# Stores of the pairs' results, the dilated attention's outputs and its statistics move from SyncE to GpSimd

## Chip, cores and metric

One core of a Trainium2 chip runs the whole program in one launch. The metric is the device time in microseconds (us), from start to end of an execution. The engines are TensorE (PE, matmuls), VectorE (DVE), ScalarE (ACT), GpSimd (POOL) and SyncE (SP). In this kernel SP starts nearly every transfer (DMA); it computes nothing.

## The reference, cut to what matters

```python
D_MODEL, SEQ, BATCH = 1024, 1024, 1
DIL_CONFIGS = ((128, 1), (512, 4), (2048, 16))   # three head groups of 4 heads, 64 channels a head
...
h = rms_norm(x, norm_w) * (1 + scale(c)) + shift(c)
proj = h @ w_in          # q,k,v,z,beta,a of mixer A; q,k,v,z of mixer B; gates g_A, g_B
...
o_a = gated_delta_rule(q_dn, k_dn, v_dn, g, beta)             # chunks of 64, 8 heads of 128
y_a = (rms_norm(o_a, dn_norm_w) * silu(za)) @ w_proj_a
...
for gi, (win, dil) in enumerate(DIL_CONFIGS):                 # mixer B: causal dilated windows
    o_g, lse_g = dilated_window_attention(qb[group], kb[group], vb[group], win, dil)
w_g = softmax(lse over the three groups)
y_b = (o_b * w_g * silu(zb)) @ w_proj_b
...
merged = sigmoid(ga) * y_a + sigmoid(gb) * y_b
x = x + gate * (merged @ w_out)
return rms_norm(x, final_norm_w)
```

All data are float32, 1024 tokens of 1024 channels.

## The kernel before

**Arithmetic.** Channels lie on the 128 partitions, tokens along the free dimension. Products of float32 matrices are split: `split` writes a rounded high part with ACT (a copy) and a low part with DVE (source minus high part), and PE makes three products (high by high, low by high, high by low).

**Buffers.** `big` holds [128, 1024] tiles, `mid` [128, 512] tiles, `wr` raw weights and `wh` split weights, all as rings of slots; `pj` and `sb` are PSUM tiles. A load that takes a slot waits until the slot's last reader is done.

**Who sets the order.** A list scheduler in Python (`Sched`) runs while the program is built. Each piece of work is a generator ("stream") with a priority. `book` keeps a modelled clock for each engine, and `run` steps the stream of the highest priority that is ready by PE's modelled clock. So the order in which instructions are written, on all engines, follows from the costs in `book`. On the chip each engine takes its instructions strictly in that order, and waits by semaphores. A changed cost in `book` can thus reorder PE, DVE, ACT and SP, though the same instructions are issued.

**The part around the change**, in the order of time:

1. Pairs (`PAIRS`, seven of them, "a" for mixer B's queries, "b" keys, "z" gates): each projects two tiles of 128 channels. `block_sink` stores each half tile [128, 512] to DRAM: `qb_d` and `kb_d` (rows `qbd`, `kbd`), `z_d` (`zd`). In the second and third head group the store also permutes tokens, in pieces of 512 x 1 x 128 or 1024 x 1 x 64.
2. Attention units (`attn_unit`, 24 of them): SP loads queries, keys and values; PE makes scores; DVE masks them and takes the row maximum; ACT takes exponentials with their sums; PE transposes; ACT copies; PE multiplies by the values; DVE copies the output; SP stores it to `og_d` (`ogd`, 128 KB). Row maxima and sums collect in `st_a` (`sta`); `attn_group` stores them after the group's last unit to `st_d` (`std`): one store for the first group, four for the second, one for the third.
3. `combine` (three): loads the statistics, forms the groups' softmax weights on DVE and ACT, transposes them and stores them to `fg_d`.
4. `yb_split` (six "slabs" of 128 channels, two per head group): loads `ogd`, `zd` and the weights (`mid<-fgd`); two half products weights x output, one whole product with z (with permuted tokens in the groups 2 and 3), then `split`. The results are the second projection's moving tiles.
5. The first projection (y_A by `w_proj_a`), eight tiles of eight steps; at each tile's end `pa_out` multiplies by a gate on DVE, `big<-big,pj`. Then the second (y_B by `w_proj_b`), eight tiles of six steps, one per slab. Weights of both are loaded and split meanwhile (`wr`, `wh`). In the last tile of the first projection the slots of its moving tiles come free step by step.

All instructions are issued through one helper, so every row of the profile has line L129; rows are told apart by engine and tile names.

Of the kernel before, what the change touches and what calls it, by code (L numbers as in the profile page):

```python
# [15 lines left out]
P = 128  # L16
# [17 lines left out]
HALVES = (slice(0, 512), slice(512, 1024))  # L34
# [13 lines left out]
def _free(ap):  # L48
    n = 1
    for s in list(ap.shape)[1:]:  # L50
        n *= s
    return n
# [83 lines left out]
class Sched:  # L136
# [19 lines left out]
    def book(self, e, op, out, a, k):  # L156
        n = _free(a[1] if op == "tensor_reduce" else out)
        done = self.cur.done
        others = max([t for q, t in done.items() if q != e], default=0.0)
        start = max(self.clk[e], self.clk["pe"], others)  # L160
        if e == "pe":
            start = self.clk["pe"]
            if op == "transpose":
                c = 109
            else:
                r = k.get("rhs", a[2] if len(a) > 2 else None)
                if r.dtype == F32R:
                    c = max(107, n / 2.4 + 2)
                elif r.shape[0] <= 64:
                    c = 30 if out.shape[0] == 32 else 60 if out.shape[0] == 64 else n / 1.1  # L170
                else:
                    c = max(214, n / 0.6) if n > 8 else 60
            end = start + c
            self.clk["pe"] = end
            hop = 190
        elif e == "dma":
            b = n * 4 * out.shape[0] * (2 if out.shape[-1] < P else 1)
            end = max(self.clk[e] + max(470, b / 360), max(self.clk["pe"], others) + 1100 + b / 360)
            self.clk[e] = end
            hop = 950  # L180
        else:
            if e == "act":
                c = n / 1.2 + (215 if "accum_out" in k else 95)
                f = TABLE.get(k.get("func", a[2] if len(a) > 2 else None))
                if f and f != self.table:
                    self.table = f
                    c += 1280
            elif e == "dve":
                c = n / 0.96 + 65
                if op == "tensor_scalar":  # L190
                    c = n / 1.92 + 130
                elif op == "scalar_tensor_tensor" and n > 8:
                    c += 60
                elif op == "reciprocal":
                    c = n * 6.2 + 70
            else:
                c = n * 2.3 + 50 if op == "tensor_tensor" else n * 1.27
                if k.get("op") == OP.pow:
                    c = n * 165 + 300
                elif n == 8 * P and k.get("op") == OP.mult:  # L200
                    c = 1900
            end = start + c
            self.clk[e] = end
            hop = 130
        done[e] = end + hop
        self.cur.last = max(self.cur.last, end + hop)
# [79 lines left out]
def hybrid_block_kernel(ctx: ExitStack, tc: tile.TileContext, x, c, norm_w, ada_w, ada_b, w_tiles, w_vb0, w_vb1,  # L286
# [3 lines left out]
    pe, act, dve, pool, sp = S.pe, S.act, S.dve, S.pool, S.sp  # L290
# [60 lines left out]
    og_d = [dp.tile([P, T], F32, name=f"ogd{i}") for i in range(6)]  # L351
# [5 lines left out]
    st_d = dp.tile([T, 3, 8], F32, name="std")  # L357
# [579 lines left out]
    def block_sink(dst, ev, func=None, scale=1.0, g=0):  # L937

        left = [2, 2]
        r_ = (1, 4, 8)[g]  # L940

        def sink(r, q, src):
            if func is not None:
                act.activation(src, src, func, scale=scale)
                yield
            if g:
                u_ = 512 // r_
                sp.dma_start(dst[r].rearrange("p (r u) -> p r u", r=r_)[:, :, q * u_:q * u_ + u_],
                             src.rearrange("p (r u) -> p r u", r=r_))
            else:  # L950
                sp.dma_start(dst[r][:, HALVES[q]], src)
            left[r] -= 1
            if not left[r]:
                S.set(ev[r])

        sink.r = r_
        return sink
# [606 lines left out]
    def attn_unit(g, i2, ti):  # L1564

        i0 = 2 * i2
        kf = max(i0 - 1, 0) if g == 0 else i0
        n_ = i0 + 2 - kf
        buf, sm2 = yield from big.many(2)
        qt, kt = buf[:, 0:256], buf[:, 256:256 + n_ * P]  # L1570
        v3 = buf[:, 640:640 + n_ * P].rearrange("p (a f) -> p a f", f=P)
        sp.dma_start(qt, qb_d[2 * g + ti][:, i0 * P:(i0 + 2) * P])
        sp.dma_start(kt, kb_d[2 * g + ti][:, kf * P:(i0 + 2) * P])
        if g == 0:
            src = vb_d[g].rearrange("(i p) f -> p i f", p=P)[:, kf:kf + n_]
        elif g == 1:
            src = vb_d[g].rearrange("(b p r) f -> r p b f", b=2, r=4)[i2]
        else:
            src = vb_d[g].rearrange("(p r) f -> p r f", r=8)[:, i0:i0 + 2]
        sp.dma_start(v3, src[:, :, ti * P:(ti + 1) * P])  # L1580
        yield
        tiles = []
        for i in (i0, i0 + 1):
            prev = (g == 0 and i > 0) or (g == 1 and i % 2 == 1)
            tiles.append((i, i % 2, (i - 1 if prev else i) - kf, 256 if prev else 128))
        sms = [sm2[:, sl] for sl in HALVES]
        pbs = yield from sb.many(2)
        for i, a, k0, nk in tiles:
            for hd in range(2):
                r = slice(64 * hd, 64 * hd + 64)  # L1590
                pe.matmul(pbs[hd][:, a * 256:a * 256 + nk], qt[r, a * P:(a + 1) * P], kt[r, k0 * P:k0 * P + nk], start=True,
                          stop=True)
        yield
        for hd in range(2):
            h4 = 2 * ti + hd
            sm = sms[hd]
            for i, a, k0, nk in tiles:
                msk = amask2 if g == 2 else amask if nk == 256 else amask[:, P:2 * P]
                dve.tensor_tensor_reduce(sm[:, a * 256:a * 256 + nk], pbs[hd][:, a * 256:a * 256 + nk], msk, -0.125, 3e38,
                                         op0=OP.add, op1=OP.min, accum_out=st_a[g][:, i, h4, 0:1])  # L1600
            sb.put()
            yield
            for i, a, k0, nk in tiles:
                s_ = sm[:, a * 256:a * 256 + nk]
                act.activation(s_, s_, AF.Exp, bias=st_a[g][:, i, h4, 0:1], scale=-1.0,
                               accum_out=st_a[g][:, i, h4, 1:2])
        yield
        pts = []
        for hd in range(2):
            pb = yield from sb.get()  # L1610
            n = 0
            for i, a, k0, nk in tiles:
                for b in range(nk // P):
                    pe.transpose(pb[:, n * P:(n + 1) * P], sms[hd][:, a * 256 + b * P:a * 256 + (b + 1) * P], ident)
                    n += 1
            yield
            pt = sms[hd]
            act.activation(pt[:, 0:n * P], pb[:, 0:n * P], AF.Copy)
            sb.put()
            pts.append(pt)  # L1620
        yield
        pb = yield from sb.get()
        n = 0
        for i, a, k0, nk in tiles:
            nb = nk // P
            for b in range(nb):
                for hd in range(2):
                    vv = v3[:, k0 + b, hd * 64:hd * 64 + 64]
                    pe.matmul(pb[64 * hd:64 * hd + 64, a * P:(a + 1) * P], vv, pts[hd][:, n * P:(n + 1) * P],
                              start=b == 0, stop=b == nb - 1)  # L1630
                n += 1
        yield
        big.put()
        dve.tensor_copy(pts[0][:, 0:2 * P], pb[:, 0:2 * P])
        sb.put()
        yield
        sp.dma_start(og_d[2 * g + ti][:, 2 * i2 * P:2 * (i2 + 1) * P], pts[0][:, 0:2 * P])
        big.put()
        pend[g] += 1
        if pend[g] == 8:  # L1640
            S.set(ev_og[g])
# [9 lines left out]
    def attn_group(g):  # L1651
        yield ev_og[g]
        sg = st_a[g]
        if g == 0:
            sp.dma_start(st_d.rearrange("(i p) g n -> p i g n", p=P)[:, :, 0], sg.rearrange("p i h s -> p i (h s)"))
        elif g == 1:
            dv = st_d.rearrange("(b p r) g n -> r p b g n", r=4, b=2)
            s4 = sg.rearrange("p (r b) h s -> p r b (h s)", b=2)
            for r in range(4):
                sp.dma_start(dv[r, :, :, 1], s4[:, r])  # L1660
        else:
            sp.dma_start(st_d.rearrange("(p i) g n -> p i g n", p=P)[:, :, 2], sg.rearrange("p i h s -> p i (h s)"))
        S.set(ev_sg[g])

    ev_sg = [Event() for _ in range(3)]
# [415 lines left out]
```

## Time and profile before

| | |
|---|---|
| time, median of 3 runs | 1279.53 us (1276.94 to 1280.24) |
| profiled execution | 1279.4 us, span 1277.7 us, granted clock 0.995 |
| PE busy | 1252.2 us (98%), 7302 matmuls |
| DVE, ACT, POOL busy | 766.9, 497.9, 173.9 us |
| stores of this change | 12 `qbd` and 12 `kbd` and 4 `zd` of 256 KB, 24 `ogd` of 128 KB, 6 `std` of 8 or 32 KB |

Busy times are shares of the span. A timeline row reads: start, duration, engine, line, operation, output <- inputs, partitions x elements, how many in a row, and in brackets the idle time of the engine before it with what ended it. PE has records with modelled ends, and a few may be missing. "SPq" is SP issuing a transfer. A row of windows gives each engine's busy time in a stretch.

### The profile page before, as it was taken

What the parts mean: (1) busy time and instruction counts of PE and PEld (TensorE: products, weight loads), DVE (VectorE), ACT (ScalarE), POOL (GpSimd) and SP (SyncE); (2) the same over time, 40 slices, a digit from 0 to 9 for tenths busy, and PEclk for the clock granted to TensorE, in tenths of its full rate; (3) what the DMA queues carried; (4) which work ended last, traced back from release to release, by engine and by line L of the source; (5) the groups of instructions that cost most, each with busy time, mean ns of one, the idle gap of its engine ahead of it and who ended that gap; (6) DMA issues with size and microseconds to landing.
All of it is one profiled execution on the core that took longest, in us unless ns stands there. A gap on an engine that the chain in (4) does not pass through costs nothing.

```text
span 1277.7 us, 19213 instructions
## 1 busy us (share of the span) xinstructions
PE 1252.2 (98%) x7302; PEld 1030.8 (81%) x7302; DVE 766.9 (60%) x1528; ACT 497.9 (39%) x1079; POOL 173.9 (14%) x128
## 2 busy tenths in 40 slices
PE   7999999999999999999999999999999999999997
PEld 3689888988888978888888888887777678878886
DVE  5845893457874367864579834555555546655533
ACT  5525622346223345233462335325555852122211
POOL 4700300033001022000320002300000000002400
PEclk9999999999999999999999999999999999999999
DMA  9534433143322262341343222645455758843422
GB/s 356 200 109 148 120 92 88 67 155 114 112 75 75 73 209 65 102 115 69 107 127 103 83 76 78 225 149 156 145 137 149 251 178 255 231 162 113 143 94 83
DMA packets 112558, 172.03 MB, mean 135 GB/s; under 512 B 41009, under 2 KB 72913, under 8 KB 112466
## 3 DMA queue, kind: packets, MB, share of 16 engines
q1 hardware_dynamic: 112322, 170.55, 42.4%
q8 instruction: 57, 0.93, 0.3%
q14 instruction: 35, 0.29, 0.1%
q10 hardware_dynamic: 144, 0.26, 0.1%
HBM read 123.40 MB, written 47.37 MB: 134 GB/s over the span
## 4 chain that ended last, share of the span: by engine, by line
PE 88%; DVE 3%; DMA 3%; ACT 2%; issue 2%; POOL 1%; SPq 0%; POOLq 0%; ACTq 0%; DVEq 0%
PE pj L129 67%; PE sb L129 22%; DVE big L129 2%; ACT big L129 1%; DMA wr<-in_w_out_dram 1%; DMA big<-kbd 1%; POOL big L129 1%; DMA big<-gd 0%; ACT wh L129 0%; DVE mid L129 0%; DVE wh L129 0%; DMA wr<-in_w_pa_dram 0%; POOL wh L129 0%; ACT L129 0%; SPq L129 0%
## 5 line engine op out<-in xcount | busy, mean ns | idle before, releaser
L129 PE MATMUL pj<-big,wh 128*128 128x512 f32 x3356 | 825.2, 398 | 0.8 <-DVE big L129 0.5
L129 PEld LDWEIGHTS pj<-big,wh 128*128 128x128 f32 x3356 | 617.2, 189 | 131.9 <-issue 9.9
L129 ACT ACTIVATE wh<-wr 128x1024 fp32r<-128x1024 f32 (+3 forms) x99 | 97.5, 985 | 239.7 <-PE pj L129 223.1
L129 DVE TENSOR_TENSOR wh<-wr,wh 128x1024 fp32r<-128x1024 f32 (+3 forms) x96 | 115.2, 1200 | 64.2 <-ACT wh L129 64.0
L129 ACT ACTIVATE big<-big 128x1024 f32<-128x1024 f32 (+2 forms) x77 | 74.1, 969 | 187.2 <-DVE big L129 133.3
L129 PE MATMUL pj<-wh,big 128*128 128x256 f32 (+2 forms) x702 | 110.6, 308 | 0.5 <-POOL wh L129 0.3
L129 PE MATMUL sb<-big,wh 128*128 128x512 f32 x368 | 105.1, 423 | 0.0
L129 PEld LDWEIGHTS pj<-wh,big 128*128 128x128 f32 x702 | 96.2, 189 | 6.2 <-POOL wh L129 0.7
L129 DVE SCALAR_TENSOR_TENSOR big<-pj,cw,big 128x1023 f32<-128x1023 f32 (+2 forms) x72 | 92.1, 1279 | 1.7
L129 PEld LDWEIGHTS sb<-big,wh 128*128 128x128 f32 x368 | 66.9, 190 | 21.1 <-issue 8.4
L129 DVE TENSOR_TENSOR big<-big,big 128x1024 f32<-128x1024 f32 (+4 forms) x44 | 57.8, 1316 | 25.9 <-ACT big L129 18.8
L129 PE MATMUL sb<-sq,big 128*128 128x128 f32 x464 | 67.9, 278 | 3.0 <-ACT sq L129 2.2
L129 PEld LDWEIGHTS sb<-sq,big 128*128 128x128 f32 x464 | 63.4, 193 | 8.8 <-ACT sq L129 3.1
L129 POOL TENSOR_TENSOR wh<-wr,wh 128x1024 fp32r<-128x1024 f32 x3 | 9.1, 3036 | 348.8 <-ACT wh L129 348.8
L129 ACT ACTIVATE big<-sb 128x512 f32<-128x512 f32 (+2 forms) x80 | 40.9, 522 | 39.6 <-PE sb L129 39.5
L129 DVE SCALAR_TENSOR_TENSOR sq<-sq,gsm,sb 128x128 f32<-128x128 f32 x48 | 16.6, 345 | 63.4 <-PE sb L129 62.2
L129 DVE CUSTOM_DVE_ANT_0 big<-sb,cst 128x128 f32<-128x128 f32 (+1 forms) x96 | 29.0, 348 | 39.7 <-PE sb L129 39.7
L129 PEld LDWEIGHTS sb<-cst,big 128*128 128x128 f32 x268 | 33.9, 145 | 22.7 <-DVE rstd L129 6.8
L129 PE MATMUL sb<-cst,big 128*128 128x128 f32 x268 | 43.5, 284 | 8.0 <-DVE rstd L129 4.9
L129 PE MATMUL pj<-big,big 128*128 128x512 f32 x210 | 49.2, 390 | 0.0
L129 ACT ACTIVATE mid<-sb 128x512 f32<-128x512 f32 (+3 forms) x48 | 24.0, 500 | 60.9 <-PE sb L129 60.5
L129 DVE TENSOR_TENSOR mid<-big 64x31 f32<-64x31 f32 (+15 forms) x124 | 41.2, 332 | 8.4 <-POOL big L129 4.9
(140 smaller groups left out, 1283.5 us busy)
## 6 DMA issues: line engine op xcount, KB each, us to landing
wr<-in_w_tiles_dram SPq DMA_DIRECT2D x64, 512.0 KB, 4.2
big<-in_ada_w_dram SPq DMA_DIRECT2D x24, 512.0 KB, 9.0
big<-in_x_dram SPq DMA_DIRECT2D x16, 512.0 KB, 5.2
gd<-big SPq DMA_DIRECT2D x16, 512.0 KB, 2.9
big<-gd SPq DMA_DIRECT2D x16, 512.0 KB, 5.2
big<-grow SPq DMA_DIRECT2D x8, 512.0 KB, 5.7
vtd<-big SPq DMA_DIRECT2D x8, 512.0 KB, 2.6
big<-vtd SPq DMA_DIRECT2D x32, 128.0 KB, 4.5
```

What stands on the lines that cost most here:

```text
L129: r = f(*a, **k)
```

## The change

58 stores are issued by POOL instead of SP: the pairs' 28, the units' 24 and the six of the statistics. `book` gets a branch for transfers on POOL: 1100 ns of the queue for an issue, landing 3000 ns and the bytes at 360 per ns after the start. Before, such a store was booked on the SP queue with that queue's cost.

```diff
@@ Sched.book
-        if e == "pe":
+        if e == "pool" and op == "dma_start":
+            self.clk[e] = start + 1100
+            end = start + 3000 + n * 4 * out.shape[0] / 360
+            hop = 950
+        elif e == "pe":
@@ block_sink
-                sp.dma_start(dst[r].rearrange("p (r u) -> p r u", r=r_)[:, :, q * u_:q * u_ + u_],
+                pool.dma_start(dst[r].rearrange("p (r u) -> p r u", r=r_)[:, :, q * u_:q * u_ + u_],
                              src.rearrange("p (r u) -> p r u", r=r_))
             else:
-                sp.dma_start(dst[r][:, HALVES[q]], src)
+                pool.dma_start(dst[r][:, HALVES[q]], src)
@@ attn_unit
-        sp.dma_start(og_d[2 * g + ti][:, 2 * i2 * P:2 * (i2 + 1) * P], pts[0][:, 0:2 * P])
+        pool.dma_start(og_d[2 * g + ti][:, 2 * i2 * P:2 * (i2 + 1) * P], pts[0][:, 0:2 * P])
@@ attn_group (three places, alike)
-            sp.dma_start(st_d..., sg...)
+            pool.dma_start(st_d..., sg...)
```

The counts of PE, DVE and ACT instructions stay. Their order changes from the third pair (about 867 us of the trace) up to the second projection's first tile (about 1124 us), and is alike before and behind.

SP's queue near the end of the attention units, before. `ogd` are output stores, `qbd`, `kbd` and `vbd` a unit's loads, `yad` loads of mixer A's output.

```order
L129 DMA ogd_190<-big_8942 128x256
L129 DMA big_9102<-qbd_179 128x256
L129 DMA big_9102<-kbd_185 128x256
L129 DMA big_9102<-vbd_119 128x2x128
L129 DMA mid_9128<-yad_126 128x512
L129 DMA mid_9129<-yad_126 128x512
L129 DMA ogd_191<-big_8978 128x256
L129 DMA big_9152<-qbd_179 128x256
L129 DMA big_9152<-kbd_185 128x256
```

Each unit's loads stand there behind an output store of an earlier unit. POOL's queue in the same part, after:

```order
L129 DMA zd_168<-mid_8651 128x512
L129 DMA zd_169<-mid_8846 128x512
L129 DMA zd_168<-mid_8799 128x512
L129 DMA ogd_189<-big_8638 128x256
L129 DMA ogd_189<-big_8686 128x256
L129 DMA ogd_190<-big_8733 128x256
L129 DMA zd_169<-mid_8719 128x512
L129 DMA std<-sta_104 128x2x8 x4
L129 DMA ogd_190<-big_8910 128x256
```

The output stores now stand among other stores only, and SP's queue holds loads there.

DVE at the last tile of the first projection, before. `pj_9742` is that tile (its row is `pa_out`), `ogd`'s slab 4 is `big_9714` with its z in `big_9715`, slab 5 `big_9769` with `big_9778`; `wh_9822` is a weight split.

```order
L129 TENSOR_TENSOR big_9714<-mid_9761,big_9714 128x512
L129 TENSOR_TENSOR big_9715<-big_9715,big_9714 128x8x128
L129 TENSOR_TENSOR big_9805<-big_9715,big_9804 128x1024
L129 SCALAR_TENSOR_TENSOR big_9740<-big_9740,pj_9742 128x1024
L129 TENSOR_TENSOR big_9769<-mid_9781,big_9769 128x512
L129 TENSOR_TENSOR wh_9822<-wr_9686,wh_9821 128x768
L129 TENSOR_TENSOR big_9769<-mid_9828,big_9769 128x512
L129 TENSOR_TENSOR big_9778<-big_9778,big_9769 128x8x128
L129 TENSOR_TENSOR big_9865<-big_9778,big_9864 128x1024
```

The same place after; slab 4 is `big_9756` with z in `big_9757`, slab 5 `big_9783` with `big_9784`, the tile `pj_9728`, the weight split `wh_9816`.

```order
L129 SCALAR_TENSOR_TENSOR big_9726<-big_9726,pj_9728 128x1024
L129 TENSOR_TENSOR wh_9816<-wr_9678,wh_9815 128x768
L129 TENSOR_TENSOR big_9783<-mid_9787,big_9783 128x512
L129 TENSOR_TENSOR big_9756<-mid_9805,big_9756 128x512
L129 TENSOR_TENSOR big_9757<-big_9757,big_9756 128x8x128
L129 TENSOR_TENSOR big_9853<-big_9757,big_9852 128x1024
L129 TENSOR_TENSOR big_9783<-mid_9843,big_9783 128x512
L129 TENSOR_TENSOR big_9784<-big_9784,big_9783 128x8x128
L129 TENSOR_TENSOR big_9865<-big_9784,big_9864 128x1024
```

Slab 4's second half product, its whole product and its split moved from ahead of the tile's gate multiply to behind it. SP's loads for these slabs, with the semaphores each waits for, before:

```order
L129 DMA big_9714<-ogd_190 128x1024 [waits DMAHW7_49]
L129 DMA big_9715<-zd_172 128x1024 [waits DMAHW0_49,DVE_49]
L129 DMA big_9769<-ogd_191 128x1024 [waits DMAHW7_49,PE_49]
L129 DMA mid_9828<-fgd_195 64x512 [waits DMAHW4_49]
L129 DMA wr_9846<-in_w_pb_dram 128x768 [waits DMAHW6_49,DVE_49]
```

and after:

```order
L129 DMA big_9756<-ogd_190 128x1024 [waits DMAHW6_49,PE_49]
L129 DMA big_9757<-zd_172 128x1024 [waits DMAHW7_49,PE_49]
L129 DMA big_9783<-ogd_191 128x1024 [waits DMAHW3_49,DMASW7_49,PE_49]
L129 DMA wr_9832<-in_w_pb_dram 128x768 [waits DMAHW2_49,DVE_49]
L129 DMA mid_9843<-fgd_195 64x512 [waits DMAHW3_49]
```

The loads of slab 4 wait for PE after the change, and the weight load stands ahead of the last load of weights `fgd` (the rows between are left out).

More of the change, by code (lines that the diff above doesn't have):

```diff
@@ L1654, in attn_group @@
         if g == 0:
-            sp.dma_start(st_d.rearrange("(i p) g n -> p i g n", p=P)[:, :, 0], sg.rearrange("p i h s -> p i (h s)"))
+            pool.dma_start(st_d.rearrange("(i p) g n -> p i g n", p=P)[:, :, 0], sg.rearrange("p i h s -> p i (h s)"))
         elif g == 1:
@@ L1659, in attn_group @@
             for r in range(4):
-                sp.dma_start(dv[r, :, :, 1], s4[:, r])
+                pool.dma_start(dv[r, :, :, 1], s4[:, r])
         else:
-            sp.dma_start(st_d.rearrange("(p i) g n -> p i g n", p=P)[:, :, 2], sg.rearrange("p i h s -> p i (h s)"))
+            pool.dma_start(st_d.rearrange("(p i) g n -> p i g n", p=P)[:, :, 2], sg.rearrange("p i h s -> p i (h s)"))
         S.set(ev_sg[g])
```

## Prediction

> **What bounds the kernel now.** I read the page's busy times, its chain and its DMA queues first.
>
> ```profile
> PE 1252.2 (98%) x7302; PEld 1030.8 (81%) x7302; DVE 766.9 (60%) x1528; ACT 497.9 (39%) x1079; POOL 173.9 (14%) x128
> ...
> q1 hardware_dynamic: 112322, 170.55, 42.4%
> ...
> PE 88%; DVE 3%; DMA 3%; ACT 2%; issue 2%; POOL 1%; SPq 0%; POOLq 0%; ACTq 0%; DVEq 0%
> ```
>
> TensorE (PE) is busy for 98% of the span and carries 88% of the chain. The change neither adds nor removes a matmul, so it can only win or lose PE's waits and what the clock does after them. SyncE's queue (SPq) has 0% of the chain: its issues as such bound nothing. So I looked next for PE's waits in the stretch that is put in another order, from the third pair (about 867 us) to the first output tile of the second projection (about 1124 us). First its list of waits for 860 to 1062 us (us in total, times, longest), then rows of PE's timeline.
>
> ```profile
> PE sb L129 <- DMA big<-kbd: 2.5, 4, 1.8
> PE sb L129 <- ACT big L129: 1.3, 2, 1.0
> ```
>
> ```profile
> 1016.17 0.71 PE L129 MATMUL sb<-cst,big 128*128 128x128 f32 x2 [1.04 <-ACT big L129]
> ...
> 1028.73 1.13 PE L129 MATMUL sb<-big 64*128 64x128 f32 x8 [1.76 <-DMA big<-kbd]
> 1029.79 4.17 PE L129 MATMUL pj<-big,wh 128*128 128x512 f32 x12
> 1033.89 0.71 PE L129 MATMUL sb<-big 64*128 64x128 f32 x8
> ...
> 1039.75 3.01 PE L129 MATMUL pj<-big,wh 128*128 128x512 f32 x12
> ...
> 1070.33 53.16 PE L129 MATMUL pj<-big,wh 128*128 128x512 f32 x232
> 1124.02 11.18 PE L129 MATMUL pj<-big,wh 128*128 128x512 f32 x48 [0.53 <-DVE big L129]
> ```
>
> Two facts carry everything below. The attention stage holds 2.5 + 1.3 = 3.8 us of PE waits, four of them for the load of an attention unit's keys. And PE waited 0.53 us at 1124.02, for the last split of an attention slab on VectorE (DVE).
>
> A wait also costs clock. After the 1.76 us, 12 matmuls took 4.17 us where 12 of the same form take 3.01, and 8 took 1.13 where 8 take 0.71: 1.16 + 0.42 = 1.6 us. The windows show it as the granted clock (behind POOL's "0.00 (x0)" stand the clock, the share of the 16 DMA engines and GB/s):
>
> ```profile
> 1024.00:1028.00 4.00, 2.71 (x18) 1.85 (x16) 1.81 (x3) 1.92 (x4) 0.00 (x0) 1.00 1.04 378
> 1028.00:1032.00 4.00, 3.27 (x13) 2.68 (x14) 2.14 (x10) 2.28 (x8) 0.00 (x0) 0.61 0.82 252
> 1032.00:1036.00 4.00, 4.00 (x25) 3.05 (x24) 1.37 (x9) 2.78 (x11) 0.00 (x0) 0.96 0.86 275
> ```
>
> The clock is 0.61 in the 4 us after that wait and 0.96 in the next. GpSimd (POOL) is at 0.00 in all three: it is free for the stores.
>
> **Part 1: 58 issues leave SP and join POOL.** What the queue held up:
>
> ```profile
> SPq L129 <- DVE big L129: 44.7, 16, 7.7
> 1021.69 0.85 SPq L129 DMA_DIRECT2D big<-kbd  x1
> 1025.00 0.32 SPq L129 DMA_DIRECT2D ogd<-big  x1
> 1048.94 0.52 SPq L129 DMA_DIRECT2D std<-sta  x1
> 1053.74 3.50 SPq L129 DMA_DIRECT2D mid<-std  x6
> 1056.94 0.85 DVE L129 TENSOR_TENSOR mid<-mid 128x32 f32<-128x32 f32 x5 [4.30 <-DMA mid<-std]
> 1080.20 1.22 DVE L129 TENSOR_TENSOR big<-big,big 128x1024 fp32r<-128x1024 f32 x1 [1.12 <-ACT big L129]
> L129 POOL TENSOR_TENSOR wh<-wr,wh 128x1024 fp32r<-128x1024 f32 x3 | 9.1, 3036 | 348.8 <-ACT wh L129 348.8
> ```
>
> An issue took SP 0.32 (an output store) to 0.52 us (a statistics store), so 58 of them free some 23 us of SP, none of it PE's. Larger is the order: between 790 and 1060 us SP stood 44.7 us waiting for DVE's `big` results with loads behind it; after the change these waits stand on POOL, with only other stores behind them. No row shows what one issue costs POOL. The nearest from below is SP's 0.32, from above POOL's longest elementwise row, 3.04 us; I take 1 us, near SP's row, since an issue passes no data through the engine. What would a late store delay? The last ones are the longest link: statistics store (1048.94), their loads (1053.74), the combination on DVE (1056.94), the first slab's split (1080.20). PE reads that slab first at the second projection's start, 32 matmuls before its wait at 1124.02, that is 1123.49 - 32 x 53.16/232 = 1116.2 us, 36 us after the split. So even 3.04 us more on the last output store, the statistics store and a landing each are hidden: 0. If a store were 10 us late or more, the chain of part 3 would start late too. For the attention units' loads the stores of their pair lie many matmuls ahead, so 0 there as well; this is the cover the third rival takes away.
>
> **Part 2: the attention stage's waits.** Loads no longer queue behind stores, so the key loads could come earlier. Against it stands the stretch where PE waited (chain; DMA in 1014 to 1032 us; the same load over the whole run):
>
> ```profile
> 1021.69 6.90 DMA big<-kbd
> ```
>
> ```profile
> q1 hardware_dynamic: 4007, 6.02, 97.0%
> big<-kbd SPq DMA_DIRECT2D x4, 128.0 KB, 4.7
> ```
>
> ```profile
> big<-kbd SPq DMA_DIRECT2D x18, 128.0 KB, 3.1
> ```
>
> The load behind the 1.76 us was issued at once, at 1021.69, 7 us ahead of its use, and took 6.90 us to land, because the transfers of that stretch fill 97% of the 16 engines; the four there took 4.7 in the median against 3.1 overall. The same bytes go through the same stretch after the change. The ends are: all 3.8 + 1.6 = 5.4 us won, or one landing of 6.90 instead of 3.1 more on the path, 3.8 us lost. I take -2.0: nearer to a gain, since SP carries loads alone, but well under half of it, since the 97% stays and PE's order puts three units' score matmuls close together.
>
> Here the Trainium skill, "DMA: Bandwidth & Descriptors", section "Issuing engines are not separate DMA queues", says that transfers issued from several engines interleave on the same 16 engines and that a second issuer saves only issue time. The trace agrees as far as it goes: 97% busy, with a wait that no issue caused. By the rule alone this part would be 0 and the sum 2.0 higher.
>
> **Part 3: the last two attention slabs.** This is the term that decides. In the new order the loads of slab 4 wait for PE, which has first to read tiles of the last tile of the first projection; before, they waited for none. So the whole of slab 4's product and split, and one more half product, now stand on DVE behind the gate multiply of that tile (`pa_out`), which waits for PE; before, slab 4 was finished ahead of it. Durations, from DVE and one ACT row before:
>
> ```profile
> 1109.56 2.17 DVE L129 TENSOR_TENSOR big<-big,big 128x1024 f32<-128x1024 f32 x1
> 1112.91 1.23 DVE L129 TENSOR_TENSOR big<-big,big 128x1024 fp32r<-128x1024 f32 x1 [1.18 <-ACT big L129]
> 1115.97 1.22 DVE L129 SCALAR_TENSOR_TENSOR big<-big,pj 128x1024 f32<-128x1024 f32 x1 [1.84 <-DMA big<-gd]
> 1117.11 0.69 DVE L129 TENSOR_TENSOR big<-mid,big 128x512 f32<-128x512 f32 x1
> 1117.71 0.95 DVE L129 TENSOR_TENSOR wh<-wr,wh 128x768 fp32r<-128x768 f32 x1
> 1118.70 0.69 DVE L129 TENSOR_TENSOR big<-mid,big 128x512 f32<-128x512 f32 x1
> 1119.43 2.18 DVE L129 TENSOR_TENSOR big<-big,big 128x1024 f32<-128x1024 f32 x1
> 1122.73 1.23 DVE L129 TENSOR_TENSOR big<-big,big 128x1024 fp32r<-128x1024 f32 x1 [1.13 <-ACT big L129]
> ```
>
> ```profile
> 1121.64 1.06 ACT L129 ACTIVATE big<-big 128x1024 fp32r<-128x1024 f32 x1 [5.27 <-DVE big L129]
> ```
>
> Before, from the gate multiply's start (1115.97) to the end of the last split (1123.96): 8.0 us. After, step by step from start to start: gate multiply 1.14, weight split 0.99, half product 0.60, half product 0.73, slab 4's product 2.21, ACT's copy 1.09, slab 4's split 1.23, half product 0.73, slab 5's product 2.21, copy 1.09, split 1.23: 13.25 us. PE already waited before, so the difference, 13.25 - 8.0 = 5.3 us, is all PE's: it would come in four pieces. Slab 4's high part is there 6.7 us after the multiply's start, and PE wants it after 24 matmuls (5.5 us): 1.2. Its low part comes 1.2 us later, when PE has done two more matmuls (0.5): 0.7. Slab 5's high part comes 4.0 after that, against four matmuls (0.9): 3.1. The last low part adds 0.8. Together 5.8 in place of 0.53. The multiply itself starts when PE ends the tile in both kernels (1116.2 by the count above, against 1115.97), so what part 2 wins moves the chain with it and doesn't shorten the wait. Ends: 3.4, if both products took the 1.23 us of a row without strides; 8.2, if one load of the chain lands 2.9 us late (a weight tile's issue, which waits for DVE's weight split, now stands ahead of the last two small loads on SP).
>
> **Part 4: clock.** The 3.1 us piece of that wait is longer than the 1.76 us that cost 1.6 us of clock: +1.6 (ends 0, since the 1.04 us wait at 1016.17 was followed by no such row, and 2).
>
> **Sum.** 0 - 2.0 + 5.3 + 1.6 = +4.9 us on the profiled execution's 1279.4 us (span 1277.7 and 1.7 around it): 1284.3 us. That execution lies 0.13 us under the median of the runs, 1279.53, so no correction. After 1124 us PE has a single wait of 0.31 us, and what follows hangs on PE's own progress: I let the delay stand to the end.
>
> **Rivals.**
> 1. The attention waits all go, and little comes in their place (no change). Part 2 is then -5.4, the sum 0 - 5.4 + 5.3 + 1.6 = +1.5, or 0 without the clock loss: 1279 to 1281 us. For it: SP waited 44.7 us ahead of loads. Against: the 97%.
> 2. Faster: the slab chain costs at most 1 us. This decides once DVE reaches slab 4's product before PE ends the last tile; then part 3 is under 1 us, part 4 is 0, and -5.4 + 1 gives 1275. For it: DVE has idle time up to the gate multiply. Against: DVE runs in order, and the product stands behind that multiply in the program.
> 3. Stores by GpSimd land late, and the loads of queries and keys that follow them too (slower by more). If POOL needs its upper 3.04 us for each, the ten stores piled up where the first split rows and the second group's statistics meet take 30 us instead of 10, and the last units' work waits for buffers that stores hold: three waits of 1.76 us are 5.3, and the sum 1289 to 1290. Against: POOL is empty there. The Trainium skill, "SBUF — State Buffer", section "SBUF: two separate sides", would push that way: it tells that DMAs of GpSimd have their descriptors written by its own cores, which VectorE's two-port operations lock out of SBUF (620 ns became 3100 ns). No run here shows a DMA of GpSimd yet.
>
> **How the numbers follow.** A measurement of this kernel tells about 0.3% (3.8 us) from no change. My forecast, slower by about 5, gets 0.45; rival 3 0.12; rival 1 0.30; rival 2 0.13. So slower 0.57, same 0.30, faster 0.13. The likeliest case alone reaches from 1282 (part 3 at 3.4) to 1287 (part 2 at 0 and the rest as taken: +6.9). The range for 8 in 10 takes rival 1 in on one side and rival 3 on the other: 1277 to 1290.
>
> **What the profile after would show.** Part 1: a GpSimd DMA queue, 58 POOL issue rows of about 1 us, and no SP row that waits for DVE with loads behind. Part 2: fewer than 3.8 us of PE waits between 860 and 1062 us, but not none, with key loads at over 4 us where the engines are full. Part 3: PE waits of 5 to 6 us in four pieces for DVE and ACT `big` in the first tile of the second projection, and two products of 2.2 us after the gate multiply. Part 4: a granted clock near 0.6 for some 4 us behind them. I am wrong if slab 4's product starts ahead of that multiply, if the attention stage loses all its waits, or if POOL's issues take 3 us.

## The result and the profile after

The changed kernel takes 1292.18 us (median of 6 runs, 1289.74 to 1295.32) against 1279.63 us before (median of 6 runs, the three of the table above among them): 12.6 us slower, ratio 1.010 with a 95% interval of 1.0083 to 1.0116. The forecast of 1284.3 us had the direction; the time lies above its range. The profiled execution took 1289.98 us, span 1287.8, granted clock 0.990.

From the page after: busy times, the two dynamic DMA queues, the chain.

```profile
PE 1257.3 (98%) x7302; PEld 1033.1 (80%) x7302; DVE 767.4 (60%) x1528; ACT 498.3 (39%) x1079; POOL 210.9 (16%) x186
...
q1 hardware_dynamic: 91426, 159.96, 38.9%
q0 software_dynamic: 3584, 10.59, 2.6%
...
PE 90%; DVE 3%; DMA 2%; ACT 2%; issue 1%; POOL 1%; SPq 0%; POOLq 0%; DVEq 0%; ACTq 0%
```

The stores moved: GpSimd has 58 instructions and 37 us more, and a queue of its own (q0). Its queue has 0% of the chain. PE has the same 7302 matmuls, but 5.1 us more busy time: the matmuls ran slower.

Where do the 10.1 us between the two profiled spans (1277.7 and 1287.8) come from? Four events stand alike in both traces and cut the span: a PE row near 451 us that waits 1.80 us for ACT `sq` (the program is the same up to 867 us), and DVE's gate multiplies of the first projection's last tile and of the second projection's first and second tile. These rows, of after first, then of before (its multiply at 1115.97 stands in the prediction):

```profile
451.81 0.49 PE L129 MATMUL sb<-sq,big 128*128 128x128 f32 x2 [1.80 <-ACT sq L129]
1118.03 1.22 DVE L129 SCALAR_TENSOR_TENSOR big<-big,pj 128x1024 f32<-128x1024 f32 x1 [2.95 <-PE pj L129]
1133.56 1.22 DVE L129 SCALAR_TENSOR_TENSOR big<-big,pj 128x1024 f32<-128x1024 f32 x1 [2.17 <-PE pj L129]
1142.83 1.22 DVE L129 SCALAR_TENSOR_TENSOR big<-big,pj 128x1024 f32<-128x1024 f32 x1 [4.43 <-PE pj L129]
```

```profile
451.39 0.49 PE L129 MATMUL sb<-sq,big 128*128 128x128 f32 x2 [1.80 <-ACT sq L129]
1125.25 1.22 DVE L129 SCALAR_TENSOR_TENSOR big<-big,pj 128x1024 f32<-128x1024 f32 x1 [1.29 <-PE pj L129]
1133.42 1.22 DVE L129 SCALAR_TENSOR_TENSOR big<-big,pj 128x1024 f32<-128x1024 f32 x1 [3.34 <-PE pj L129]
```

| stretch | before | after | difference |
|---|---|---|---|
| start to the PE row near 451 us | 451.39 | 451.81 | +0.42 |
| to the first projection's last gate multiply ("attention stretch") | 664.58 | 666.22 | +1.64 |
| to the second projection's first one ("slab stretch") | 9.28 | 15.53 | +6.25 |
| to its second one | 8.17 | 9.27 | +1.10 |
| to the end of the span | 144.3 | 145.0 | +0.7 |

So 7.35 of 10.1 us arise where the last two attention slabs meet the second projection, and 1.64 in the attention stretch.

**The attention stretch after.** PE's timeline, then PE's list of waits for 860 to 1062 us:

```profile
1016.71 1.23 PE L129 MATMUL sb<-big 64*128 64x128 f32 x8 [3.40 <-DMA big<-kbd]
...
1019.31 1.23 PE L129 MATMUL sb<-big 64*128 64x128 f32 x8 [0.33 <-DMA big<-kbd]
```

```profile
PE sb L129 <- DMA big<-kbd: 3.7, 2, 3.4
PE sb L129 <- ACT big L129: 0.5, 1, 0.5
```

The four waits for keys (2.5 us) became two (3.7 us), one of them 3.40 us long, and 8 score matmuls behind each took 1.23 us (0.71 at full clock). Why the keys were late shows in SP's queue (timeline) and in its waits between 995 and 1018 us:

```profile
1001.84 4.41 SPq L129 DMA_DIRECT2D wr<-in_w_pa_dram  x2
...
1006.78 0.42 SPq L129 DMA_DIRECT2D big<-kbd  x1
...
1010.48 0.50 SPq L129 DMA_DIRECT2D big<-kbd  x1
...
1013.31 0.80 SPq L129 DMA_DIRECT2D big<-kbd  x1
```

```profile
SPq L129 <- DVE wh L129: 11.1, 2, 7.4
```

SP no longer stands behind stores here. It stands behind two loads of weights that wait for a slot, which DVE's weight split frees (`DVE wh`, 11.1 us in two waits). Behind them came three units' loads in a bunch, while the DMA engines were full (their share was 0.95 and 1.03 in 1008 to 1016, and it stayed there; windows, the last three columns are the clock, the DMA share and GB/s):

```profile
1016.00:1020.00 4.00, 2.96 (x18) 2.40 (x20) 2.06 (x10) 2.06 (x10) 0.00 (x0) 0.53 1.08 388
1020.00:1024.00 4.00, 4.00 (x23) 2.88 (x21) 2.64 (x12) 4.00 (x16) 0.00 (x0) 0.62 1.03 389
```

**The slab stretch after.** PE's timeline, DVE's, and the windows:

```profile
1124.64 0.73 PE L129 MATMUL pj<-big,wh 128*128 128x512 f32 x2 [1.22 <-ACT big L129]
1125.90 1.20 PE L129 MATMUL pj<-big,wh 128*128 128x512 f32 x4 [0.52 <-DVE big L129]
1130.19 61.56 PE L129 MATMUL pj<-big,wh 128*128 128x512 f32 x258 [3.08 <-ACT big L129]
```

```profile
1119.16 0.95 DVE L129 TENSOR_TENSOR wh<-wr,wh 128x768 fp32r<-128x768 f32 x1
1120.03 1.29 DVE L129 TENSOR_TENSOR big<-mid,big 128x512 f32<-128x512 f32 x2
1121.36 2.15 DVE L129 TENSOR_TENSOR big<-big,big 128x1024 f32<-128x1024 f32 x1
1124.62 1.22 DVE L129 TENSOR_TENSOR big<-big,big 128x1024 fp32r<-128x1024 f32 x1 [1.12 <-ACT big L129]
1126.32 0.69 DVE L129 TENSOR_TENSOR big<-mid,big 128x512 f32<-128x512 f32 x1 [0.47 <-DMA mid<-fgd]
1127.05 2.00 DVE L129 TENSOR_TENSOR big<-big,big 128x1024 f32<-128x1024 f32 x1
1130.17 1.23 DVE L129 TENSOR_TENSOR big<-big,big 128x1024 fp32r<-128x1024 f32 x1 [1.12 <-ACT big L129]
```

```profile
1128.00:1132.00 4.00, 1.78 (x3) 1.00 (x4) 2.27 (x2) 1.06 (x1) 0.00 (x0) 0.61 0.00 0
1132.00:1136.00 4.00, 4.00 (x11) 3.13 (x10) 2.41 (x3) 0.84 (x1) 0.00 (x0) 0.54 0.00 0
1136.00:1140.00 4.00, 4.00 (x19) 3.28 (x18) 2.13 (x3) 1.06 (x1) 0.00 (x0) 1.00 0.50 153
```

Behind the gate multiply at 1118.03 stand both slabs' products and splits, in the forecast order, to 1131.40. PE waits 1.22, 0.52 and 3.08 us for them, and the clock stays at 0.61 and 0.54 until 1136.

### The profile page after: what moved, and what is told of

The parts are those of the page before. It is cut to its first block, busy times and chain, and to the rows that moved or that the text cites. A ratio compares the mean times of both kernels' runs of the same rounds, so it can differ in the third digit from the quotient of the medians.

```text
span 1287.8 us, 19245 instructions
## 1 busy us (share of the span) xinstructions
PE 1257.3 (98%) x7302; PEld 1033.1 (80%) x7302; DVE 767.4 (60%) x1528; ACT 498.3 (39%) x1079; POOL 210.9 (16%) x186
## 4 chain that ended last, share of the span: by engine, by line
PE 90%; DVE 3%; DMA 2%; ACT 2%; issue 1%; POOL 1%; SPq 0%; POOLq 0%; DVEq 0%; ACTq 0%
PE pj L129 68%; PE sb L129 23%; DVE big L129 2%; ACT big L129 1%; DMA wr<-in_w_out_dram 1%; POOL big L129 1%; DMA big<-vbd 0%; DMA big<-kbd 0%; DMA mid<-fgd 0%; ACT wh L129 0%; DVE wh L129 0%; DVE mid L129 0%; POOL wh L129 0%; ACT junk L129 0%; SPq L129 0%
## 5 line engine op out<-in xcount | busy, mean ns | idle before, releaser
L129 ACT ACTIVATE big<-big,sta 128x128 f32<-128x128 f32 (+1 forms) x96 | 42.1, 441 | 15.5 <-DVE sta L129 13.4
L129 PEld LDWEIGHTS pj<-big,big 128*128 128x128 f32 x210 | 39.3, 188 | 8.8 <-POOL big L129 0.6
```

What stands on the lines that cost most here:

```text
L129: r = f(*a, **k)
```

## Experiments

Ratios are against the kernel before, timed beside each. The "slab sum" is the slab stretch and the next together: 17.45 us before, 24.80 after.

**The written order without GpSimd.** The order of after, with the 58 stores booked as POOL's but issued by SP.

```diff
+        self.st = Engine(self, nc.sync, "pool")
-        pool.dma_start(...)          # the 58 stores
+        S.st.dma_start(...)
```

> The written order of the changed kernel (its booking), but the 58 stores issued by SP again, at the same places of the order. Order theory (the loss is made by the new order of loads and DVE work, whoever issues the stores): ratio to before 1.008 to 1.012, with the 13 us chain of the last two slabs and PE waits of 4 to 5 us at the second projection's first tile. GpSimd theory (the loss is made by stores that land later from GpSimd's queue): ratio about 1.000, with the waits at that tile under 1 us.

1294.42 us, 1.0118 (1.0081 to 1.0155); slab sum 24.13 us, attention stretch 668.96 us, with 6.9 us of waits for keys between 860 and 1062 us (3.7 after). The loss is there in full without a single store on GpSimd.

**GpSimd without the new order.** The stores on POOL, booked as SP's were, so that the order of before is written.

```diff
-        if e == "pool" and op == "dma_start":
-            ...
+        self.st = Engine(self, nc.gpsimd, "dma")
-        pool.dma_start(...)
+        S.st.dma_start(...)
```

> The order of the kernel before (booked as before), but the 58 stores issued by GpSimd. Order theory: ratio 0.997 to 1.001; the PE waits of the attention stage (3.8 us before) go down to between 0.5 and 4 us, since SP holds loads alone but the transfers still fill the 16 engines, and the wait at the second projection's first tile stays near 0.5 us. GpSimd theory: ratio 1.006 to 1.012, with later stores and new waits behind them.

1278.73 us, 1.000 (0.998 to 1.002), profiled 1276.81 us; slab sum 17.34 us. PE's timeline:

```profile
1016.24 0.71 PE L129 MATMUL sb<-cst,big 128*128 128x128 f32 x2 [1.10 <-ACT big L129]
...
1120.29 58.34 PE L129 MATMUL pj<-big,wh 128*128 128x512 f32 x256 [0.52 <-DVE big L129]
```

No wait for keys is left, the clock is 1.00 in every 4 us window from 860 to 1062 us, and the attention stretch takes 660.45 us against 664.58. With this order the move does what Part 2 had hoped for. The same kernel again, to see whether it wins:

> The order of before with the stores issued by GpSimd once more, in five rounds: its profile was 3.0 us shorter than that of before, its median 0.4. If the 2.4 us of vanished waits for keys and their clock loss are real, the ratio is 0.996 to 0.999; if they are given back elsewhere, 1.000.

1279.67 us, 0.9991 (0.9974 to 1.0008), attention stretch 659.18 us. The stretch is shorter in both profiles by 4 to 5 us, yet the time is not measurably lower. The start to the PE row near 451 us, before anything has changed, took 451.91 us in the one and 456.56 us in the other profile; such scatter may hide a gain of that size, but what swallowed it isn't settled.

**Filling PE's waits**, to part the wait from the clock: products of no use ahead of slabs 4 and 5 in the second projection's first tile, first 4 and 12, then 10 and 10.

```diff
+                if j == 0 and kk >= 4:
+                    dum = sbp.tile([P, 512], F32, tag="sb", name=f"dum{kk}")
+                    for _ in range((4, 12)[kk - 4]):      # then: range(10)
+                        nc.tensor.matmul(dum, u.hi[:, 0:P], YB[0][0][:, 0:512], start=True, stop=True)
```

> The changed kernel with 4 and 12 extra matmuls on data at hand, ahead of the steps of slab 4 and slab 5 in the second projection's first tile, where PE idles 1.2 and 3.1 us; their results are used by nothing. If idle time lowers the clock (about 3.9 us lost behind these waits by the matmul durations), the granted clock there stays near 1.0 and the time falls by 3 to 4 us against the changed kernel (ratio to before 1.006 to 1.008). If the low clock comes from something else, the time stays (1.010).

1294.17 us, 1.0116 (1.0082 to 1.0149): no gain. PE's timeline:

```profile
1132.36 0.73 PE L129 MATMUL pj<-big,wh 128*128 128x512 f32 x2 [2.15 <-ACT big L129]
...
1134.66 4.46 PE L1926 MATMUL dum<-big,wh 128*128 128x512 f32 x12
```

A first wait of 2.15 us was left behind four products, since slab 4 was ready later here (DVE waited 1.49 us for a load of `fgd`). The 12 products behind it ran at the low clock, 4.46 us where 12 take 3.01. The second wait was gone, but the slab sum, 24.79 us, didn't move.

> As the filling of 4 and 12, but 10 and 10 extra matmuls, so that PE has work from before the first wait of the second projection's first tile. Clock theory (a wait of over 1 us lowers the clock for the microseconds behind it, whether PE works in them or not): with the first wait covered the clock stays at 1.0, the stretch from the last gate multiply of the first projection to the second gate multiply of the second, 24.8 us in the changed kernel and with 4 and 12, falls to 21.5 to 23. Against it: if the extra matmuls only take the place of waits, it stays at 24.5 to 25.

1292.01 us, 1.0089 (1.0068 to 1.011); slab sum 25.50 us. Ten products didn't cover the first wait either, since here slab 4 was later (DVE's timeline):

```profile
1127.35 0.69 DVE L129 TENSOR_TENSOR big<-mid,big 128x512 f32<-128x512 f32 x1 [2.57 <-DMA mid<-fgd]
```

PE waited 1.95 us more and the clock fell again (0.81 and 0.76 in 1132 to 1140 us). Neither run parts the cost of the clock from the wait.

**Less work on DVE.** The z products of slabs 4 and 5 are left out (two of DVE's 2 us rows).

```diff
-            dve.tensor_tensor(perm(z, g), perm(z, g), og..., op=OP.mult)
+            if j >= 4:
+                S.book("dve", "tensor_tensor", perm(z, g), (perm(z, g),), {})
+            else:
+                dve.tensor_tensor(perm(z, g), perm(z, g), og..., op=OP.mult)
```

> The changed kernel without the two DVE products with z of slabs 4 and 5 (2.2 us each, left out of the computation; the order stays). Chain theory (the DVE chain behind the last gate multiply sets PE's waits at that tile): the waits fall from 4.8 us to under 1.5, the clock loss behind them goes, the time falls by 6 to 8 us (ratio 1.003 to 1.005). If loads, not DVE, set these waits, they stay at 3 us or more and the time falls by less than 3 us.

1288.57 us, 1.007 (1.0045 to 1.0095); slab sum 21.41 us, 3.4 less than after. DVE's chain carries a part of it; then the loads of the weights `fgd` bind, as DVE's timeline shows:

```profile
1129.58 0.69 DVE L129 TENSOR_TENSOR big<-mid,big 128x512 f32<-128x512 f32 x1 [2.30 <-DMA mid<-fgd]
```

**Fewer bytes beside the key loads.** Two 512 KB gate loads are issued later (their slots stay booked), against the theory that full DMA engines make the keys late.

```diff
+        if j < 2:
+            S.book("dma", "dma_start", t, (t,), {})
+            late[j] = t          # issued in the first projection, tile j, step 4
+        else:
+            sp.dma_start(t, gate_d[j])
```

> The changed kernel, with the loads of the first two gate tiles (512 KB each) issued on SP behind the last units' loads, not among them. Full-engine theory (the keys come late because the transfers of that stretch fill the 16 engines): the wait of 3.4 to 4.4 us for keys near 1016 us falls to under 2.5 and the stretch from 451 us to the last gate multiply of the first projection, 666 to 668 us in the changed kernel, shortens by 1.5 us or more. Blocked-queue theory (the keys come late because SP stands 4.4 us before a weight load, with the units' loads behind it): the wait stays above 3 us.

1291.62 us, 1.0097 (1.0069 to 1.0126); attention stretch 666.12 us. The DMA engines stayed as full without these two loads (1.02 and 1.05 in 1016 to 1024 us), so this run does not decide the theory. PE still waited:

```profile
1015.11 0.71 PE L129 MATMUL sb<-big 64*128 64x128 f32 x8 [2.95 <-DMA big<-kbd]
```

**The blocking load behind the units' loads.** The other theory: the fourth weight load of the first projection, which waits for its slot, is issued after the three units' loads.

```diff
+            if u is pa_units[3]:
+                S.book("dma", "dma_start", u.raw, (u.raw,), {})
+                late.append(u)       # issued after the loads of unit (2, 0, 3)
+            else:
+                sp.dma_start(u.raw, u.src)
```

> The changed kernel, with one weight load (the fourth tile of the first projection, on which SP stands for 4.4 us near 1002 us until VectorE has freed its slot) issued behind the loads of three attention units, not ahead of them. Blocked-queue theory: the units' loads are issued about 4 us earlier, the wait for keys near 1016 us falls from 3.4 to 4.4 us to under 1, with its clock loss, and the time falls by 4 to 6 us (ratio to before 1.005 to 1.007). Full-engine theory: loads are issued earlier but land as late, the wait stays above 2 us and the time changes by under 2 us.

1289.26 us, 1.0069 (1.0048 to 1.0091); attention stretch 662.62 us, 3.6 less than after. SP's queue, PE's timeline and a window:

```profile
1004.12 0.43 SPq L129 DMA_DIRECT2D big<-kbd  x1
...
1006.54 0.42 SPq L129 DMA_DIRECT2D big<-kbd  x1
...
1009.73 0.32 SPq L129 DMA_DIRECT2D big<-kbd  x1
```

```profile
1017.32 0.71 PE L129 MATMUL sb<-cst,big 128*128 128x128 f32 x2 [1.10 <-ACT big L129]
1018.27 0.71 PE L129 MATMUL sb<-big 64*128 64x128 f32 x8 [0.24 <-DMA big<-kbd]
```

```profile
1016.00:1020.00 4.00, 2.60 (x19) 1.55 (x19) 2.62 (x14) 3.72 (x16) 1.41 (x2) 1.00 1.04 405
```

Nothing about the bytes changed (the engines are as full, and the key loads still took 6.1 us to land in the median of 1000 to 1030 us), only the place of one load in the queue: the key loads were issued 2.7 to 3.9 us earlier in a trace that is 2.5 us late at the row near 451 us, and the wait for keys fell from 3.7 to 0.24 us. Five waits for ACT, 3.2 us in all, took most of its place, so PE's waits fell only from 4.2 to 3.4 us. Most of the 3.6 us is the clock, which stayed at 1.00 where after had lost 2.9 us (worked out below). The slab sum was 25.52 us, 0.7 more than after, and the two ratios' intervals just overlap: the stretch shows the gain better than the time does.

**Both together** (the last edit and the left-out z products):

> The changed kernel with both edits at once: the weight load issued behind the three units' loads, and no DVE products with z of slabs 4 and 5 (left out of the computation). If the two terms are separate places of the chain, the gains add: the stretch from 451 us to the last gate multiply of the first projection near 662.6 us, from there to the next 12 us, the time 7 to 9 us under the changed kernel (ratio to before 1.002 to 1.005). If the one only moves the wait to the other, the sum stays at 1.006 or more.

1285.36 us, 1.0047 (1.0029 to 1.0066); attention stretch 665.09 us, slab sum 21.43 us. The slab sum repeats the 3.4 us. Of the 3.6 us in the attention stretch only 1.1 came back here, so its size is known to a few us only. PE's timeline shows a reason, and something else about the clock:

```profile
1020.71 1.23 PE L129 MATMUL sb<-big 64*128 64x128 f32 x8 [0.60 <-DMA big<-kbd]
...
1127.00 1.65 PE L129 MATMUL pj<-big,wh 128*128 128x512 f32 x6 [2.03 <-DVE big L129]
1131.14 19.11 PE L129 MATMUL pj<-big,wh 128*128 128x512 f32 x83 [2.49 <-DVE big L129]
```

Behind a wait for ACT of 1.10 us, the wait for keys was 0.60 us here, not 0.24, and the clock was 0.57 in 1020 to 1024: of the 3.40 us of PE's busy time there some 1.5 are lost. At the slabs PE waited 2.03 and 2.49 us, longer than with the left-out products alone (0.43 and 2.47), but the clock stayed at 1.00 behind both; there it fell to 0.58 in 1132 to 1136. So the same sum came about in two ways.

**Other prices, other orders.** The changed kernel with other numbers in the new branch of `book`: 550 for 1100 and 2000 for 3000, and then 550 and 1100.

```diff
-            self.clk[e] = start + 1100
-            end = start + 3000 + n * 4 * out.shape[0] / 360
+            self.clk[e] = start + 550
+            end = start + 2000 + ...        # the second: start + 1100
```

> The changed kernel, booked with 550 ns for an issue and 2000 ns to landing in place of 1100 and 3000, which is nearer to the issue that the trace showed (0.54 to 0.86 us). The order is another one, with slab 4's product still behind the gate multiply. Chain theory: the stretch from that multiply to the next is 15 to 16.5 us again and the time is over that of before (ratio 1.005 to 1.010). If only the exact order of the change was bad luck, 1.000.

1290.03 us, 1.009 (1.0059 to 1.0121); attention stretch 663.02, slab sum 25.43 us. Slab 4 stays behind the gate multiply here.

> Booked with 550 ns for an issue and 1100 ns to landing. A third order, in which slab 4's product and split stand ahead of the gate multiply, as before the change, and all 58 stores are on GpSimd. Chain theory: 9.2 us from gate multiply to gate multiply, as before; with the units' loads free of stores the waits for keys are under 2 us, so the ratio is 0.996 to 1.002. If orders of this kind are worse in other places too, it is over 1.004.

1280.57 us, 1.0007 (0.9993 to 1.0021); slab sum 17.31 us. Here slab 4 stands ahead of the multiply, and PE's timeline has:

```profile
1019.98 0.95 PE L129 MATMUL sb<-big 64*128 64x128 f32 x8 [2.04 <-DMA big<-kbd]
...
1121.99 18.20 PE L129 MATMUL pj<-big,wh 128*128 128x512 f32 x79 [0.53 <-DVE big L129]
```

The same 58 stores on the same engine, another written order, and the loss is gone. No kernel here beats the one before by more than its interval.

## Why the prediction was right or wrong

**The main claim held**: the loss comes from the written order, and the issuing engine costs nothing that can be told. The two runs that part them (1.0118 and 1.000) show it.

**Part 1, taken as 0: right.** An issue took GpSimd in the mean 0.56 us (the output stores) to 0.79 us (the statistics), under the 1 us taken. Rows of GpSimd and of its DMA issues after, then the same issues before (KB each, median us to landing):

```profile
L129 POOL DMA_DIRECT2D ogd<-big x24 | 13.4, 558 | 68.0 <-DVE big L129 47.3 <-issue 15.0 <-DVE sta L129 4.0
L129 POOL DMA_DIRECT2D qbd<-mid x12 | 8.7, 723 | 62.6 <-DVE mid L129 60.0 <-DVE big L129 2.6
L129 POOL DMA_DIRECT2D std<-sta x6 | 4.7, 788 | 0.0
```

```profile
ogd<-big POOLq DMA_DIRECT2D x24, 128.0 KB, 4.0
```

```profile
ogd<-big SPq DMA_DIRECT2D x24, 128.0 KB, 2.6
```

They land later, as the third rival had it, but by 1.4 us (0.8 in the run with the order of before, whose 1.000 shows nothing of it). The Trainium skill, "SBUF — State Buffer", section "SBUF: two separate sides", tells of descriptor writing by GpSimd that VectorE's two-port operations lock out, so that a transfer of 620 ns took 3100 ns. No issue that has a row of its own took over 0.97 us here, and the landings grew by 1.4 us, so no run here shows such a price. The Trainium skill, "DMA: Bandwidth & Descriptors", section "Issuing engines are not separate DMA queues", grants a second issuer only the issue time; the 1.000 of the whole time agrees, the waits for keys, which did go in that order, don't.

**Part 2, -2.0: the step that failed.** "Since SP carries loads alone" the keys were to come earlier. In the order of before that is true (attention stretch 4 to 5 us shorter). In the order of after, a weight load that waits for DVE took the stores' place at the head of SP's queue. Such waits were there to be seen: between 860 and 1062 us SP stood 22.2 us for `DVE wh` before and 59.4 us after. Their total doesn't decide (41.9 us in the order of before with the stores on GpSimd, without a wait for keys), but which loads stand behind them. The working of this part: waits 3.7 + 0.5 = 4.2 us, and at 0.53 and 0.62 of the clock the 2.96 and 4.00 us of PE's busy time in 1016 to 1024 lost 1.4 + 1.5 = 2.9: 7.1 in place of 3.8 + 1.6 = 5.4, so +1.7; the anchors say +1.64. The four profiles that have the program of after up to the gate multiply (after, the two fillers, the left-out product) give 666.22, 668.29, 666.62 and 667.24 us, mean 667.1 or +2.5. The term was off by 3.6 to 4.5 us. The 97% of the engines, which made me stop at -2.0, did not decide: the share is 1.04 in the run where the wait went. It makes the landings long (5.5 us in the median for the keys of 1000 to 1030 us after, 6.1 in that run), but loads that are issued early enough cover that.

**Part 3, +5.3: mechanism right, size near.** Gate multiply to last split took 13.4 us (forecast 13.25). PE's waits were 1.22 + 0.52 + 3.08 = 4.82 us in place of 0.53, so +4.3. The forecast's fourth piece, 0.8 us, has no row: PE was still in its slow matmuls. One link of the chain was not in the forecast's sum, only in its upper end: the chain after, which ends in the longest wait, runs through a load of `fgd`, issued behind a weight load.

```profile
1120.15 0.34 SPq L129
...
1121.04 5.18 DMA mid<-fgd
```

DVE waited 0.47 us for it (the row at 1126.32 above), and 2.57 and 2.30 us for such loads in the second filler and with the z products left out; so leaving the z products out gave 3.4 us, not all of it. DVE's own work and this load ended within 0.47 us of each other: that DVE's durations alone came so near to 13.4 us was in part luck.

**Part 4, +1.6: too small by half.** The slab stretch grew by 6.25 us, 1.96 more than its waits, and the next by 1.10 us without a wait: 3.1 us of slower matmuls. The windows agree: of the 5.8 us of PE's busy time in 1128 to 1136 at 0.61 and 0.54, some 2.5 us are lost; the other 0.6 is not attributed. The forecast carried over the price of a 1.76 us wait; the 3.08 us wait, with two smaller ones just before, kept the clock low for some 6 us of work, not 4. What sets this price is not shown: with both edits, waits of 2.03 and 2.49 us at the same place cost no clock.

**The sum.** Forecast 0 - 2.0 + 5.3 + 1.6 = +4.9. Measured between the profiles: 0 + 1.64 + 4.3 + 3.1 = +9.0, and 1.1 us from the start and the end, which no part had. So of the 5.2 us by which the forecast was short, 3.6 are Part 2 and 1.5 Part 4, and Part 3 was 1.0 too large. The medians differ by 12.6 us: the profile of after lies 2.2 us under its median, of which the mean of the attention stretch explains 0.9; the rest is not attributed. Rivals 1 and 2 fell with the waits that stayed. The median lies even above rival 3's 1289 to 1290, and its cause, issues of 3.04 us, is not there. None of the three signs named as "I am wrong if" appeared: a weight load that blocks the attention units' loads was not among the cases considered.

## What to carry to other kernels

When a scheduler's cost table is edited, run the edit in two halves: the new engine with the old order, and the new order with the old engine. Here the first gave 1.000 and the second 1.0118. For a queue that is relieved, ask what stands at its head next: a load that waits for a slot blocks the loads behind it as well as a store does. Moving one such load took PE's waits for keys from 3.7 to 0.24 us; other waits gave most of that back, but the clock loss behind it was gone.

## What the runs showed of the hardware

- A wait of PE can cost clock besides its own time, but its length alone doesn't set the price. 3.40 us made two groups of 8 matmuls take 1.23 us each (0.71 at full clock), with clocks of 0.53 and 0.62 over 8 us; 2.04 us made the next 8 take 0.95, with 0.57 over 4 us. 1.10 and 0.24 us near each other left a clock of 1.00, but 1.10 and 0.60 us were followed by 0.57; and 2.03 and 2.49 us at another place left it at 1.00. The Trainium skill, "TensorE: Matmul & The Clock Gate", section "Part 1: The HAM clock gate (the "warmup" mystery)", speaks of an idle window of about 3.4 us before the clock is halved; here the clock fell behind 2.04 us and, before the change, 1.76 us.
- Work given to PE after such a wait runs at the low clock too (12 products in 4.46 us): it doesn't buy the clock back at once.
- The same program takes 450.5 to 456.6 us to one and the same early PE row, from profile to profile. A gain of 4 us in one stretch can stay below what the whole time tells.
